# The low parts of the weight units are subtracted on GpSimd in place of VectorE, in a hybrid decoder layer

## The chip, the cores and the metric

One core of one Trainium2 chip runs the whole kernel. The metric is the device time of one execution in microseconds (us). TensorE (PE in the profile) multiplies matrices; VectorE (DVE), ScalarE (ACT) and GpSimd (POOL) do the elementwise work; SyncE (SP) and GpSimd issue most of the transfers between memory and SBUF. Each engine takes its instructions from a queue of its own, strictly in order; an instruction that has to wait holds all that stand behind it.

## What is computed

One layer for two groups of requests that share the weights: a prompt of 1024 positions and 8 sequences of 8 new positions, T = 1088 columns together. The model width is 1024, the feed-forward width 2816. Everything is float32.

```python
xn = rmsnorm(x)
q, k, v, a, b, gate_a, gate_b = split(xn @ w_in)           # 5632 columns
A = window_attention(q, k, v, sinks) @ w_o_attn            # 16 heads, 4 kv heads, window 128
u = a * sigmoid(b)
B = silu(layernorm(depthwise_conv31(u))) @ w_pb
h = x + (sigmoid(gate_a) * A + sigmoid(gate_b) * B) @ w_out
up = depthwise_conv3(rmsnorm(h) @ w_up)                    # 2 * 2816 columns
gate, val = split(up)
y = rmsnorm(h + (silu(gate) * val) @ w_down)
```

Key and value caches and convolution states are outputs as well.

## The kernel before

**How a product is made.** TensorE multiplies in a float format (`F32R`) that keeps fewer bits than float32. So each operand x is held as a pair: a high part, x rounded to that format, and a low part, x minus the high part. `mm3` (L188 to L192) makes a product from three matmuls into the same PSUM bank: high weight by high input (L190), high weight by low input (L191), and low weight by high input (L192). Of the three only L192 reads the low part of the weights, and it comes last.

**Weight units.** The weights arrive as units of 128x1024, each the weights for 128 output columns. A unit passes through four steps. `w_load` (L143) has it read from memory into a raw tile by SyncE's queue, two or three units ahead. `w_parts` (L156) makes the pair: ScalarE casts the raw tile to the high part (L171), and an engine subtracts the high part from the raw tile to give the low part (L172). The pair lies in one of two buffers that take turns (`slot`, L175), so a cast has to wait until TensorE has finished with the unit that held the buffer. `stream` (L194) then runs the three matmuls for all columns of the input, chunk by chunk. `weight` (L178) has the next unit split while the present one is multiplied: one unit ahead. `w_split` (L151) makes the split of a unit in two halves for the first five units (`FIRST = 5`), in one piece of 1024 columns for all others. Lines after L172 have a number higher by one in the kernel after the change.

**Stages.** The times are those of the profiled execution, rounded.

- 0 to 640 us: the input projection, 44 units in the order of `SEQUENCE`, 1088 columns each in chunks of 384, 384 and 320. Its results leave PSUM through small copies (L739 for q, for instance). Each of eight pairs of units b and a yields 128 channels for the long convolution, `conv` (L508), which is elementwise work on VectorE: some sixty operations of 512 columns (L520 and L526 to L542) for a group of 128 channels, here called a channel for short. At its end two DMA instructions of GpSimd's queue (L543, L544) store the result to `d_c`. The convolution is put behind more urgent work by 1200 steps of priority (`CONV_LATER`), so that it fills VectorE's gaps and comes late. In between, attention runs in units: scores on TensorE, `softmax` (L359) on VectorE and ScalarE with one small copy of the sinks on GpSimd (L362), transposes, and the product with the values.
- 640 to 736 us: the attention's output projection, 8 units, together with the layer norm of the convolution's result.
- 736 to 830 us and 831 to 930 us: the projections `w_pb` and `w_out`, 8 units each, and the second norm.
- 930 to 1003 us: the first three pairs of feed-forward up-projection units (`plain`), in quarters of 272 columns. Before each unit's results, `up_start` (L1144) has GpSimd clear and fill the edges of the tile (L1152); afterwards `finish` (L1175) runs the short convolution: `up_conv` copies two small edges on GpSimd (L1167 and the line after it), ScalarE makes the first tap (L1170), VectorE the other two (L1172), and GpSimd stores the product. VectorE also makes sums of the inputs (L1223) in this stretch, for what follows.
- 1003 to 1405 us: the other up-projection pairs, by a scheme with seven products of half-size blocks in place of eight. The weight blocks of this scheme are split by other lines (`split_ps`, L225 and L226), which the change does not touch; GpSimd negates a half tile here (L1196).
- 1405 to 1662 us: the down-projection and the last norm. Ten of its units are split by L171 and L172, again in tiles that other data held before; the rest by other lines.

**What sets the order.** The program is written in one sequence, and each instruction has a priority from its place in it. `later(off)` puts a block behind by so many places; `plan` and `tick` insert attention steps between matmuls. A scheduler then places the instructions in each engine's queue from these priorities and its own estimates of when operands are ready. So an instruction that changes its engine changes the order of its neighbours as well. Tiles that take turns in a buffer make an instruction wait for the last reader of the buffer.

Of the kernel before, what the change touches and what calls it, by code (L numbers as in the profile page):

```python
# [6 lines left out]
F32 = mybir.dt.float32  # L7
F32R = mybir.dt.float32r
AF = mybir.ActivationFunctionType
ALU = mybir.AluOpType  # L10
# [42 lines left out]
FIRST = 5  # L53
# [67 lines left out]
class Build:  # L121
# [34 lines left out]
    def w_parts(self, m):  # L156
        i = len(self.w_hl)
        r = self.w_raw[i]
        pool, x = self.slot(i)
        if pool is None:  # L160
            h, l = x
        else:
            th, tl = x if isinstance(x, tuple) else (f"whi{x}", f"wlo{x}")
            n = 2 if th == tl else 1
            h = self.t(pool, [P, DM], th, F32R, bufs=n)
            l = self.t(pool, [P, DM], tl, F32R, bufs=n)
        self.w_hl.append((h, l))

        def part(x):
            z = slice(x * DM // m, (x + 1) * DM // m)  # L170
            self.cast = self.nc.scalar.copy(h[:, z], r[:, z]).ins  # L171
            self.nc.vector.tensor_tensor(l[:, z], r[:, z], h[:, z].bitcast(F32), ALU.subtract)  # L172
        return [lambda x=x: part(x) for x in range(m)]

    def slot(self, i):  # L175
# [1502 lines left out]
```

## Time and profile before

| what | value |
|---|---|
| time of the runs | 1665.16 and 1667.07 us, median 1666.12 us |
| span of the profiled execution | 1662.4 us |
| TensorE busy | 1652.5 us (99%) |
| VectorE busy | 1337.3 us (80%) |
| ScalarE busy | 866.3 us (52%) |
| GpSimd busy | 290.2 us (17%) |
| mean DMA rate | 113 GB/s |

The span runs from the first to the last instruction that the profiler records. The rest of a run's time, 3.7 us of the median, lies outside it. A row of a timeline has the start in us, the duration in us, engine, line, operation, the tiles written and read, their shapes, how many instructions the row holds, and in brackets the time that the engine waited before it and what ended the wait. A row of a group has the line, engine, operation, tiles, shapes and count; behind the first bar the busy time in us and the mean of one in ns, behind the second the idle time of the engine just before these instructions.

### The profile page before, as it was taken

To read this page: it belongs to the slowest core of one execution; us is meant where nothing else is said; L and a number is where in the kernel's file an instruction comes from. 1 tells how busy PE (TensorE), PEld (TensorE's weight loads), DVE (VectorE), ACT (ScalarE), POOL (GpSimd) and SP (SyncE) were. 2 spreads that over 40 slices of the span, in tenths; PEclk is the share of its full clock that TensorE was granted. 3 is DMA by queue.
4 is the path that set the end of the run, shared out by engine and by line. 5 is a ranking of instruction groups with operands and counts; after the bars stand their busy time and mean duration, and the time that the engine had idled before them with its cause. 6 is when DMAs were issued, how large, how long until landed. Compare 5 with 4: busy or idle time off the path is not lost.

```text
span 1662.4 us, 29877 instructions
## 1 busy us (share of the span) xinstructions
PE 1652.5 (99%) x11550; PEld 1636.9 (98%) x11550; DVE 1337.3 (80%) x2432; ACT 866.3 (52%) x1781; POOL 290.2 (17%) x483
## 2 busy tenths in 40 slices
PE   9999999999999999999999999999999999999998
PEld 9999999999999999999999999999999999999997
DVE  7899979999989986855545896777887786988867
ACT  6424368774488845973233454444444454524222
POOL 0100112231011111110000171344444320000000
PEclk9999999999999999999999999999999999999999
DMA  6221212232121265544343332244444324766403
GB/s 208 84 71 42 75 60 81 99 103 86 55 53 48 77 227 168 178 154 145 106 155 108 80 125 103 97 113 115 112 114 111 94 103 134 243 168 168 118 14 108
DMA packets 98623, 187.09 MB, mean 113 GB/s; under 512 B 22848, under 2 KB 57680, under 8 KB 98464
## 3 DMA queue, kind: packets, MB, share of 16 engines
q1 hardware_dynamic: 79152, 125.18, 24.3%
q0 software_dynamic: 18896, 59.72, 11.9%
q8 instruction: 91, 1.49, 0.4%
q14 instruction: 52, 0.43, 0.1%
q10 hardware_dynamic: 432, 0.27, 0.1%
HBM read 129.75 MB, written 57.35 MB: 113 GB/s over the span
## 4 chain that ended last, share of the span: by engine, by line
PE 91%; DVE 5%; ACT 2%; DMA 1%; issue 1%; ACTq 0%; DVEq 0%; SPq 0%
PE mm L190 23%; PE mm L192 23%; PE mm L191 23%; PE aux L190 6%; PE aux L192 6%; PE aux L191 6%; PE aux L406 1%; DVE c L520 1%; PE aux L418 1%; PE aux L419 1%; PE aux L396 1%; PE aux L397 1%; DVE bt L520 1%; DVE q L739 1%; DMA bw<-d_b 0%
## 5 line engine op out<-in xcount | busy, mean ns | idle before, releaser
L190 PE MATMUL mm<-xh,whi 128*128 128x384 f32 (+1 forms) x904 | 301.1, 333 | 0.0
L191 PE MATMUL mm<-xl,whi 128*128 128x384 f32 (+1 forms) x904 | 295.4, 327 | 0.1
L192 PE MATMUL mm<-xh,wlo 128*128 128x384 f32 (+1 forms) x904 | 295.4, 327 | 0.0
L191 PEld LDWEIGHTS mm<-xl,whi 128*128 128x128 f32 x904 | 170.0, 188 | 1.6 <-DVE xl L277 0.7
L190 PEld LDWEIGHTS mm<-xh,whi 128*128 128x128 f32 x904 | 169.8, 188 | 0.7
L192 PEld LDWEIGHTS mm<-xh,wlo 128*128 128x128 f32 x904 | 169.7, 188 | 0.1
L190 PE MATMUL mm<-mh,whi 128*128 128x272 f32 (+4 forms) x428 | 125.9, 294 | 0.0
L191 PE MATMUL mm<-ml,whi 128*128 128x272 f32 (+4 forms) x428 | 125.1, 292 | 0.0
L192 PE MATMUL mm<-mh,wlo 128*128 128x272 f32 (+4 forms) x420 | 123.5, 294 | 0.0
L1172 DVE SCALAR_TENSOR_TENSOR acc<-st,fc,acc 128x1104 f32<-128x1104 f32 x88 | 119.8, 1364 | 2.8 <-ACT acc L1170 2.0
L171 ACT CAST whi<-wraw 128x1024 fp32r<-128x1024 f32 (+1 forms) x76 | 74.2, 981 | 79.8 <-PE mm L191 59.7
L520 DVE SCALAR_TENSOR_TENSOR bt<-u,consts,bt 128x513 f32<-128x513 f32 x120 | 89.8, 748 | 0.7
L520 DVE SCALAR_TENSOR_TENSOR c<-sm,hsum,c 128x512 f32<-128x512 f32 x120 | 89.6, 747 | 0.7
L172 DVE TENSOR_TENSOR wlo<-wraw,whi 128x1024 fp32r<-128x1024 f32 (+1 forms) x76 | 86.1, 1136 | 4.9 <-ACT whi L171 4.6
L520 DVE SCALAR_TENSOR_TENSOR c<-u,consts,c 128x512 f32<-128x512 f32 x112 | 83.7, 747 | 0.5
L190 PEld LDWEIGHTS mm<-mh,whi 128*128 128x128 f32 x428 | 80.5, 188 | 0.2
L191 PEld LDWEIGHTS mm<-ml,whi 128*128 128x128 f32 x428 | 80.6, 188 | 0.0
L192 PEld LDWEIGHTS mm<-mh,wlo 128*128 128x128 f32 x420 | 79.0, 188 | 0.0
L1152 POOL COPY st<-co 128x16 f32<-128x16 f32 x44 | 75.6, 1724 | 0.2 <-issue 0.2
L191 PE MATMUL mm<-tl,whi 128*128 128x272 f32 x240 | 69.6, 290 | 0.0
L1320 ACT COPY st<-mm 128x272 f32<-128x272 f32 (+2 forms) x133 | 44.6, 349 | 47.8 <-PE mm L192 47.8
L192 PE MATMUL mm<-th,whi 128*128 128x272 f32 x240 | 69.3, 289 | 0.0
(462 smaller groups left out, 5491.6 us busy)
## 6 DMA issues: line engine op xcount, KB each, us to landing
wraw<-wall SPq DMA_DIRECT2D x118, 512.0 KB, 3.8
bw<-d_b SPq DMA_DIRECT2D x42, 272.0 KB, 3.4
d_b<-gd POOLq DMA_DIRECT2D x36, 272.0 KB, 6.1
d_b<-acc POOLq DMA_DIRECT2D x24, 272.0 KB, 3.3
ar<-wdn SPq DMA_DIRECT2D x32, 192.0 KB, 4.3
d_g<-acc POOLq DMA_DIRECT2D x10, 544.0 KB, 4.3
ga<-d_ga SPq DMA_DIRECT2D x8, 544.0 KB, 4.0
gb<-d_gb SPq DMA_DIRECT2D x8, 544.0 KB, 3.6
```

Of the source, the lines that this page charges most:

```text
L171: self.cast = self.nc.scalar.copy(h[:, z], r[:, z]).ins
L172: self.nc.vector.tensor_tensor(l[:, z], r[:, z], h[:, z].bitcast(F32), ALU.subtract)
L190: mm(ps, wh, xh, start=first, stop=False, skip_group_check=more)
L191: mm(ps, wh, xl, start=False, stop=False, skip_group_check=more)
L192: mm(ps, wl, xh, start=False, stop=last, skip_group_check=more)
L396: nc.tensor.matmul(ps[:, j, :], q[g][:, h, qs], kd[g][:, keys], start=True, stop=False)
L397: nc.tensor.matmul(ps[:, j, :], q[g][:, h, qs], kl[g][:, keys], start=False, stop=True)
L406: nc.tensor.transpose(ps[:, h * P:(h + 1) * P], pt[:, h, kb * P:(kb + 1) * P], self.ident)
L520: mac = lambda o, x, w: nc.vector.scalar_tensor_tensor(o, x, w, o, ALU.mult, ALU.add)
L1152: nc.gpsimd.tensor_copy(ss[:, :, 0:2], co[:, f, 2:].rearrange("p (b t) -> p b t", b=NB))
L1172: nc.vector.scalar_tensor_tensor(acc, st[:, k:k + AW], fw(f, k), acc, ALU.mult, ALU.add)
L1320: op(d, r(ps))
```

## The change

From the sixth weight unit on, the low part is subtracted by GpSimd; the first five units stay on VectorE. Nothing else is edited: the same operands, the same tiles, the same cast on ScalarE.

```diff
         def part(x):
             z = slice(x * DM // m, (x + 1) * DM // m)
             self.cast = self.nc.scalar.copy(h[:, z], r[:, z]).ins
-            self.nc.vector.tensor_tensor(l[:, z], r[:, z], h[:, z].bitcast(F32), ALU.subtract)
+            low = self.nc.vector if i < FIRST else self.nc.gpsimd
+            low.tensor_tensor(l[:, z], r[:, z], h[:, z].bitcast(F32), ALU.subtract)
         return [lambda x=x: part(x) for x in range(m)]
```

Here `i` is the number of the unit in the order of use and `m` the number of pieces. 39 subtractions of the input projection, 24 of the three projections behind it, 6 of the first up-projection units and 10 of the down-projection change their engine: 79 operations of 128x1024.

## The prediction

> **What bounds the kernel now.** I read the page first, then TensorE's waits, then the windows of the stages in which VectorE is densest, then the timelines around each place where a moved subtraction gets a neighbour in its new queue.
>
> ```profile
> PE 1652.5 (99%) x11550; PEld 1636.9 (98%) x11550; DVE 1337.3 (80%) x2432; ACT 866.3 (52%) x1781; POOL 290.2 (17%) x483
> PE mm L629 <- DVE warm L622: 1.1, 1, 1.1
> PE mm L190 <- DVE H L1456: 0.9, 1, 0.9
> PE aux L418 <- ACT pth L225: 0.8, 1, 0.8
> 60.00:460.00 400.00, 399.90 (x2577) 395.60 (x2576) 372.26 (x698) 223.53 (x525) 61.20 (x120) 1.00 0.25 76
> 964.00:978.50 14.50, 14.50 (x117) 14.50 (x117) 14.50 (x24) 6.65 (x12) 10.81 (x2) 1.00 0.55 188
> ```
>
> TensorE (PE) is busy for 1652.5 of 1662.4 us: 9.9 us are idle in all, and none of its listed waits is over 1.1 us. So help to any other engine can win at most 9.9 us, 0.6%. A window's columns are its length, then PE, weight loads, VectorE (DVE), ScalarE (ACT) and GpSimd (POOL) busy, then PE's granted clock (1.00: full) and the DMA. VectorE comes next: 372.3 of 400 us from 60 to 460, and no pause at all from 964 to 978.5.
>
> ```profile
> L172 DVE TENSOR_TENSOR wlo<-wraw,whi 128x1024 fp32r<-128x1024 f32 x29 | 35.4, 1220 | 0.4 <-ACT whi L171 0.2
> 759.68 1.05 ACT L171 CAST whi<-wraw 128x1024 fp32r<-128x1024 f32 x1 [1.57 <-PE mm L191]
> 771.59 1.05 ACT L171 CAST whi<-wraw 128x1024 fp32r<-128x1024 f32 x1 [1.62 <-issue]
> ```
>
> The first row is the subtraction from 60 to 460 us: 29 of them at 1.22 us. The others are two casts, each made when PE leaves a weight buffer. Units follow at 11.9 us; less the cast, some 10.8 us remain to make the low part. That slack hides a slower subtraction if it starts when its cast ends.
>
> **The change, part by part.** The built program's order shows 79 subtractions of 128x1024 gone from VectorE's queue and the same 79 in GpSimd's. The matmuls stay; VectorE's and GpSimd's other work is placed anew around them.
>
> *One subtraction on GpSimd.* No row shows a two-input operation there. The nearest:
>
> ```profile
> 1076.91 0.69 DVE L226 TENSOR_TENSOR wlo<-wraw,wlo 128x512 fp32r<-128x512 f32 x1 [0.86 <-ACT wlo L225]
> 1077.23 1.81 POOL L1196 TENSOR_SCALAR gd<-acc 128x544 f32<-128x544 f32 x1
> 1077.52 0.43 DVE L1296 TENSOR_TENSOR st<-st,aux 128x272 f32<-128x272 f32 x1
> 966.68 2.63 DVE L1223 TENSOR_TENSOR s<-mh,ml 128x544 f32<-128x544 f32 x4
> 968.28 10.46 POOL L1167 COPY co<-st 128x2 f32<-128x2 f32 x1 [3.17 <-ACT st L1163]
> 978.62 1.37 DVE L1172 SCALAR_TENSOR_TENSOR acc<-st,fc,acc 128x1104 f32<-128x1104 f32 x1
> ```
>
> The scalar operation ends 1.43 us after VectorE's L226 (1076.91+0.69=1077.60 to 1079.04). For 1024 columns in place of 544 that is 2.7 us. Lower bound: VectorE's 1.22. Upper: 5.4, if a second input doubles it. I take 2.7, the row's own rate. The Trainium skill, "GPSIMD Engine Reference", section 3.1, gives 4497 ns for a two-input add of 2048 fp32 columns; 2.25 us for 1024 is an estimate by that page, and the sum below would be about 13 us in place of 24.
>
> *What the two engines cost each other.* A copy of two columns took 10.46 us at 968.28: VectorE ran two-input operations on SBUF without a gap, and the copy ended at 978.74, just after the first L1172. So GpSimd's reads wait for such a stream and get in ahead of an operation with per-partition scalars (L1172). The reverse, VectorE held by GpSimd, no row shows: the operations with one operand in PSUM (L1296) ran beside L1196 in 0.43 us, as elsewhere. Its bounds are nothing and the whole 2.7 us. By its nearest row, the copy, the exclusion is complete, so I take it as mutual. The Trainium skill says the same, "SBUF — State Buffer", section "Who interferes with whom": a VectorE instruction with two SBUF inputs contends with a GpSimd instruction that reads SBUF, and the later one fully blocks. The trace agrees for one direction (10.46 us); by that rule VectorE pays nearly the whole 2.7.
>
> ```profile
> L520 DVE SCALAR_TENSOR_TENSOR bt<-u,consts,bt 128x513 f32<-128x513 f32 x90 | 67.4, 748 | 0.6
> L520 DVE SCALAR_TENSOR_TENSOR c<-sm,hsum,c 128x512 f32<-128x512 f32 x90 | 67.2, 747 | 0.6
> L520 DVE SCALAR_TENSOR_TENSOR c<-u,consts,c 128x512 f32<-128x512 f32 x84 | 62.8, 747 | 0.5
> L526 DVE TENSOR_TENSOR c<-u,consts 128x992 f32<-128x992 f32 x12 | 14.2, 1185 | 0.1
> L528 DVE TENSOR_TENSOR sm<-u 128x527 f32<-128x527 f32 x6 | 4.2, 705 | 0.0
> L540 DVE TENSOR_TENSOR c<-c,bt 128x512 f32<-128x512 f32 x6 | 4.1, 687 | 0.0
> L542 DVE TENSOR_TENSOR u<-c,bt 128x512 f32<-128x512 f32 x6 | 4.1, 683 | 0.0
> ```
>
> From 60 to 460 us these steps with two SBUF inputs, all of the convolution, fill 224 of the 336.9 us (372.3 less 35.4) that VectorE keeps: two thirds. So the loss per subtraction lies between 1.8 (two thirds of 2.7) and 2.7 in this stage; I take the middle, 2.3, against 1.22 saved. VectorE gets busier, not freer.
>
> *First place: the sixth convolution channel.*
>
> ```profile
> 440.54 0.55 DVE L739 TENSOR_TENSOR q<-mm,q 64x384 fp32r<-64x384 f32 x1
> 444.14 0.34 PE L192 MATMUL mm<-xh,wlo 128*128 128x384 f32 x1
> 453.24 0.69 DVE L541 TENSOR_TENSOR u<-c 128x512 f32<-128x512 f32 x1
> 454.23 0.54 POOL L543 DMA_DIRECT2D d_c<-u  x1 [5.91 <-DVE u L541]
> ```
>
> In the new GpSimd queue the low part that PE needs at 444.14 stands behind this channel's two stores, and those wait for VectorE's L541, done at 453.9. Ahead of that L541 VectorE now has 40.1 us less (35.4 of 29 subtractions, 4.7 of 26 small operations placed later) and 29 holds more: at 2.3 us each 66.7. It can fill the 27.7 us that it idled: 453.9-40.1+66.7-27.7=452.8. Then 0.2 to start, 0.54 for the store, 2.7 for the subtraction: 456.2, PE 12 us late. With a hold of 1.8 the channel ends with the evacuation placed ahead of it (L739 at 440.54, then four short steps, 442.5), so PE is 1 or 2 us late; with 2.7 it is 24. Smaller collisions of this kind, with the first, second and fifth channels, lie inside the same delay, since PE that is late needs its weights later. Behind the waiting stores stand only the next subtractions and the next channel's memsets.
>
> *460 to 640 us.*
>
> ```profile
> 460.00:550.00 90.00, 89.15 (x580) 85.76 (x579) 81.19 (x194) 76.04 (x192) 12.39 (x25) 1.00 0.18 50
> 550.00:640.00 90.00, 90.00 (x568) 88.32 (x567) 73.79 (x144) 48.74 (x110) 14.93 (x29) 1.00 0.51 176
> L362 POOL COPY p<-nsink 128x4 f32<-128x4 f32 x32 | 14.1, 444 | 74.6 <-PE aux L406 69.9 <-ACT gt L222 4.1 <-PE mm L191 0.7
> ```
>
> VectorE has 25 us idle here; about twelve subtractions add 12x1.1=13: hidden, 0 (up to 10). The softmax's sink copies (L362) now queue behind subtractions, whose cover is the time PE gives to other matmuls: 2 us (0 to 8).
>
> *640 to 940 us.* Output projections: the slack of 10.8 us holds, and nothing late stands ahead in the queue: 0.
>
> *Second place: the first up-projection units.*
>
> ```profile
> 951.80 1.05 ACT L171 CAST whi<-wraw 128x1024 fp32r<-128x1024 f32 x1 [1.91 <-PE mm L191]
> 955.00 0.29 PE L192 MATMUL mm<-mh,wlo 128*128 128x272 f32 x1
> 953.28 1.31 ACT L1170 ACTIVATE acc<-st,fc 128x1104 f32<-128x1104 f32 x1
> 955.35 1.36 DVE L1172 SCALAR_TENSOR_TENSOR acc<-st,fc,acc 128x1104 f32<-128x1104 f32 x1
> 979.22 0.29 PE L192 MATMUL mm<-mh,wlo 128*128 128x272 f32 x1
> 981.80 1.37 DVE L1172 SCALAR_TENSOR_TENSOR acc<-st,fc,acc 128x1104 f32<-128x1104 f32 x1
> 985.63 1.22 DVE L172 TENSOR_TENSOR wraw<-wraw,wraw 128x1024 fp32r<-128x1024 f32 x1
> 986.76 2.77 DVE L1172 SCALAR_TENSOR_TENSOR acc<-st,fc,acc 128x1104 f32<-128x1104 f32 x2
> ```
>
> Here slack is small: cast done at 952.85, low part wanted at 955.00. VectorE streams, so the subtraction gets in ahead of the first L1172 (now as soon as ScalarE's L1170 is done, 954.6) and ends at 957.3: 2.3 us late. In the new queue the low part for 979.22 stands behind two such copies, a memset and three stores, one entry per L1172: the copies take those at 978.62 and 981.8, it takes the third (986.76; with the subtraction of 985.63 gone, at about 985.6), and ends at 988.3: 9 us late, which holds the first delay. Entry in an earlier gap: 5. One miss more: 16.
>
> *Third place, the down-projection.*
>
> ```profile
> 1399.39 1.23 DVE L172 TENSOR_TENSOR ml<-wraw,mh 128x1024 fp32r<-128x1024 f32 x1 [1.25 <-ACT mh L171]
> 1405.34 0.33 PE L192 MATMUL mm<-mh,whi 128*128 128x384 f32 x1
> ```
>
> Two subtractions follow each other from 1399.4: the second ends at 1404.8, wanted at 1405.34. I put 1 us (0 to 3).
>
> **Sum.** 12+0+2+9+1=24 us on the profiled execution's 1662.4: 1686.4. The runs' median, 1666.1, stands 3.7 above that span: **1690**.
>
> **Rivals.** *A, hidden:* at the input projection VectorE loses less than the 1.22 us it saves, so the sixth channel is done by 441 and nothing queues late; at the up-projection subtractions get in at once. Then VectorE's relief may take PE's 0.9 and 0.8 us waits too, and the sink copies cost 2 at most: 1664 to 1668, not slower. It decides at a hold below about 1.2 us. For it: the 10.8 us of slack, and no row with VectorE held. Against: the 10.46 us copy.
> *B, the subtraction is long:* 5.4 us with a hold of 4.6 gives 453.9-40.1+133-27.7=519 at the sixth channel, 78 us late with the longer subtraction; then 12x3.4-25=16, and 16 at the up-projection: 1776. Half-way from my case to that: 1735.
> *C, starved further:* two subtractions at the up-projection miss the L1172s and wait, as the copy at 968.28 did, 10.46 us each: 1690+21=1711. For it: that copy. Against: the sink copies (L362) between the convolution's steps took 444 ns on average.
> *D, relief pays:* all of PE's 9.9 us, 1656; but most of those lie in no wait for VectorE. The change cannot fail to do what it says: the queues show it.
>
> **Chances.** 2% (33 us, 1699.4 above and 1632.8 below) is about what a measurement of this kernel can tell from no change. Forecast 0.50, of which 0.41 lies within 2%; A 0.17; B 0.20, all slower; C 0.12, of which 0.02 within; D 0.01. Together: slower by over 2% 0.39, within 0.60, faster 0.01 as a bound on what I overlooked. The forecast's own range runs from its low ends together (1+0+0+5+0=6: 1672) to 1712, where the high ends no longer come together. For 8 in 10 it takes in A down to 1665 and B to 1745, a little past its half-way case.
>
> **What would show it.** Right: GpSimd busy up by 79x2.7=213 us or more, PE idle near 34 us, with waits of L192 matmuls for GpSimd around 455 and 980; L520 longer or later after a subtraction. Wrong: subtractions of 5 us, or PE without waits for GpSimd (A), or long subtraction spans outside the convolution (C).

## The result and the profile after

| | median of the runs | profiled span | PE busy | VectorE busy | GpSimd busy |
|---|---|---|---|---|---|
| before | 1666.12 us | 1662.4 us | 1652.5 us | 1337.3 us | 290.2 us |
| after | 1720.72 us | 1717.2 us | 1671.0 us | 1367.7 us | 481.6 us |

The changed kernel is slower: 1719.03 to 1722.41 us, ratio 1.0324 with a 95% interval of 1.0291 to 1.0356. That is 54.6 us more, where 23.9 were forecast. (To the kernel's description above: the first three units are split in quarters, not in halves; they keep their engine.)

These lines of the page of the changed kernel answer to those of before (lines of code from L173 on stand one lower than in the kernel before, so L521 is the convolution step that was L520):

```profile
PE 1671.0 (97%) x11550; PEld 1645.2 (96%) x11550; DVE 1367.7 (80%) x2353; ACT 866.1 (50%) x1781; POOL 481.6 (28%) x562
PE 69%; DVE 23%; ACT 5%; issue 2%; DMA 1%; POOL 0%; DVEq 0%; ACTq 0%; SPq 0%; POOLq 0%
L173 POOL TENSOR_TENSOR wlo<-wraw,whi 128x1024 fp32r<-128x1024 f32 x68 | 183.1, 2693 | 260.9 <-ACT whi L171 227.1
L521 DVE SCALAR_TENSOR_TENSOR bt<-u,consts,bt 128x513 f32<-128x513 f32 x120 | 111.4, 928 | 0.6
L521 DVE SCALAR_TENSOR_TENSOR c<-sm,hsum,c 128x512 f32<-128x512 f32 x120 | 101.9, 849 | 0.5
L521 DVE SCALAR_TENSOR_TENSOR c<-u,consts,c 128x512 f32<-128x512 f32 x112 | 97.3, 869 | 0.6
```

VectorE has 79 operations fewer and is busy 30.4 us longer. The convolution steps show where: the same instruction that took 748 or 747 ns on average now takes 849 to 928. The second line is the chain that ended last: VectorE has 23% of it, GpSimd nothing. In the kernel before VectorE had 5%:

```profile
PE 91%; DVE 5%; ACT 2%; DMA 1%; issue 1%; ACTq 0%; DVEq 0%; SPq 0%
```

Now TensorE's waits in the changed kernel:

```profile
PE aux L420 <- DVE ptl L227: 8.9, 7, 3.2
PE aux L562 <- DVE red L555: 6.1, 3, 2.3
PE aux L397 <- DVE ptl L227: 4.9, 3, 3.1
PE mm L191 <- ACT st L1164: 5.2, 2, 2.7
PE mm L191 <- ACT qs L745: 3.3, 3, 1.2
PE mm L191 <- DVE H L1457: 2.5, 5, 0.7
PE mm L193 <- POOL wlo L173: 0.8, 1, 0.8
```

The columns are the total in us, how often, and the longest. TensorE waited for a low part once, for 0.8 us. It waits for VectorE's attention steps (L227), for the layer norm's sums (L555), and for ScalarE's copies out of PSUM (L1164, L745).

**One hold.** The timelines of GpSimd and VectorE at 150 us:

```profile
150.05 2.76 POOL L173 TENSOR_TENSOR wlo<-wraw,whi 128x1024 fp32r<-128x1024 f32 x1 [11.99 <-ACT whi L171]
149.79 0.76 DVE L521 SCALAR_TENSOR_TENSOR bt<-u,consts,bt 128x513 f32<-128x513 f32 x1
150.47 2.89 DVE L521 SCALAR_TENSOR_TENSOR c<-u,consts,c 128x512 f32<-128x512 f32 x1
153.28 0.74 DVE L521 SCALAR_TENSOR_TENSOR c<-sm,hsum,c 128x512 f32<-128x512 f32 x1
```

The subtraction runs from 150.05 to 152.81. The convolution step that starts in this time takes 2.89 us in place of 0.75; the step behind it takes 0.74 again. VectorE was held for 2.1 us.

**Where the time went.** I compared each VectorE instruction that overlaps a subtraction with the median of the same instruction in the trace before; where it took over 0.3 us longer I call the difference a hold. The delay is the start of the same matmul in both traces, after less before, so it is exact for these two executions (stretches by the times of the trace before):

| stretch, us | subtractions | with a hold | holds, us | delay added, us | forecast, us |
|---|---|---|---|---|---|
| 60 to 460 | 30 | 23 | 46.9 | 24.8 | 12 |
| 460 to 640 | 11 | 8 | 13.6 | 9.3 | 2 |
| 640 to 736 | 7 | 7 | 14.3 | 8.6 | 0 |
| 736 to 930 | 17 | 13 | 24.5 | 0.0 | 0 |
| 930 to 1003 | 4 | 4 | 8.3 | 9.2 | 9 |
| 1003 to 1405 | 2 | 0 | 0 | 0.0 | 0 |
| 1405 to the end | 8 | 6 | 9.3 | 2.7 | 1 |
| sum | 79 | 61 | 116.9 | 54.6 | 24 |

Holds come at some 2 us each in all stretches but one. What they cost differs: nothing from 736 to 930, more than their length from 930 to 1003. Of the 2.7 us behind 1405 about half is no effect of the change: fill and only_pb_out (below), which have no GpSimd subtraction there, lose 1.3 and 1.4 us in this stretch against the same trace.

Of the 54.8 us by which the span grew, 36.3 are TensorE's idle time (46.2 in place of 9.9). Another 8.5 or so are a lower granted clock after such stops: 17 us at 0.50. The remaining ten lie in matmuls that the profile shows as longer; they were not taken apart.

### The profile page after: what moved, and what is told of

Same layout as the page of the kernel before. It is cut to its first block, busy times and chain, and to the rows that moved or that the text cites. A ratio compares the mean times of both kernels' runs of the same rounds, so it can differ in the third digit from the quotient of the medians.

```text
span 1717.2 us, 29881 instructions
## 1 busy us (share of the span) xinstructions
PE 1671.0 (97%) x11550; PEld 1645.2 (96%) x11550; DVE 1367.7 (80%) x2353; ACT 866.1 (50%) x1781; POOL 481.6 (28%) x562
## 4 chain that ended last, share of the span: by engine, by line
PE 69%; DVE 23%; ACT 5%; issue 2%; DMA 1%; POOL 0%; DVEq 0%; ACTq 0%; SPq 0%; POOLq 0%
PE mm L191 16%; PE mm L193 16%; PE mm L192 16%; DVE c L521 6%; PE aux L191 5%; PE aux L193 5%; PE aux L192 5%; DVE bt L521 4%; DVE s L1224 1%; ACT p L374 1%; DVE q L740 1%; DVE c L527 1%; DVE p L369 1%; DVE c L528 1%; PE aux L407 1%
## 5 line engine op out<-in xcount | busy, mean ns | idle before, releaser
L173 POOL TENSOR_TENSOR wlo<-wraw,whi 128x1024 fp32r<-128x1024 f32 x68 | 183.1, 2693 | 260.9 <-ACT whi L171 227.1
L1173 DVE SCALAR_TENSOR_TENSOR acc<-st,fc,acc 128x1104 f32<-128x1104 f32 x88 | 124.1, 1411 | 13.3 <-ACT acc L1171 12.4
L521 DVE SCALAR_TENSOR_TENSOR bt<-u,consts,bt 128x513 f32<-128x513 f32 x120 | 111.4, 928 | 0.6
L521 DVE SCALAR_TENSOR_TENSOR c<-sm,hsum,c 128x512 f32<-128x512 f32 x120 | 101.9, 849 | 0.5
L521 DVE SCALAR_TENSOR_TENSOR c<-u,consts,c 128x512 f32<-128x512 f32 x112 | 97.3, 869 | 0.6
L374 ACT ACTIVATE p<-p,nm 128x257 f32<-128x257 f32 (+1 forms) x128 | 62.3, 490 | 23.2 <-DVE nm L369 20.9
L1153 POOL COPY st<-co 128x16 f32<-128x16 f32 x44 | 71.7, 1636 | 0.2 <-issue 0.2
```

Source lines behind the costliest of these rows:

```text
L173: low.tensor_tensor(l[:, z], r[:, z], h[:, z].bitcast(F32), ALU.subtract)
L374: nc.scalar.activation(pt[:, j, lo:width + 1], pt[:, j, lo:width + 1], AF.Exp, bias=nm[:, j:j + 1], scale=-1.0, accum_out=den[:, j:j + 1])
L521: mac = lambda o, x, w: nc.vector.scalar_tensor_tensor(o, x, w, o, ALU.mult, ALU.add)
L1153: nc.gpsimd.tensor_copy(ss[:, :, 0:2], co[:, f, 2:].rearrange("p (b t) -> p b t", b=NB))
L1173: nc.vector.scalar_tensor_tensor(acc, st[:, k:k + AW], fw(f, k), acc, ALU.mult, ALU.add)
```

## The experiments

The theory after the first look: a GpSimd instruction that reads SBUF holds a VectorE instruction with two inputs from SBUF until it is done, and the held time reaches TensorE through VectorE's fixed queue (**holds**). The rivals: VectorE's queue was placed anew by the scheduler, 515 of its 2294 entries other than the subtractions, and the new order is worse (**order**); or low parts come late in GpSimd's queue (**queue**). The first three kernels take these apart two by two: the old and the new order on VectorE, each with GpSimd reading and not reading.

**fill**: new order, no reads.

```diff
-            low = self.nc.vector if i < FIRST else self.nc.gpsimd
-            low.tensor_tensor(l[:, z], r[:, z], h[:, z].bitcast(F32), ALU.subtract)
+            if i < FIRST:
+                self.nc.vector.tensor_tensor(l[:, z], r[:, z], h[:, z].bitcast(F32), ALU.subtract)
+            else:
+                self.nc.gpsimd.memset(l[:, z].bitcast(F32), 0.0)
```

> In place of the subtraction GpSimd fills the low part with zeros (units from the sixth on): it writes the same tile but reads nothing, so the low parts of these weights are left out of the result. VectorE's queue is that of the changed kernel, with 9 of 2294 entries elsewhere. Theory 1, holds (a GpSimd subtraction reads SBUF and holds VectorE's operations that have two SBUF inputs): no read, no hold, so the 54.6 us vanish: 1660 to 1669 us. Theory 2, order (VectorE's queue was placed anew, 515 of 2294 entries, and its evacuations of PSUM now stand behind convolution steps): the order is still there, so 1700 to 1725 us. Theory 3, queue (the low part comes late in GpSimd's queue, behind stores): a fill is shorter than a subtraction but stands at the same place, so about half of the loss, 1680 to 1700 us.

**twice**: old order, reads that nobody waits for (the diff is against the kernel before).

```diff
             self.nc.vector.tensor_tensor(l[:, z], r[:, z], h[:, z].bitcast(F32), ALU.subtract)
+            if i >= FIRST:
+                self.nc.gpsimd.tensor_tensor(r[:, z], r[:, z], h[:, z].bitcast(F32), ALU.subtract)
```

> VectorE subtracts as in the kernel before, in nearly its order (25 of 2294 entries elsewhere), and GpSimd then makes the same subtraction once more, into the raw tile that nobody reads any more. No matmul waits for GpSimd. Theory 1, holds: VectorE keeps its 79 subtractions (some 96 us) and pays the holds besides (the trace of the changed kernel shows some 115 us of them), so at least the loss of the changed kernel: 1720 to 1800 us, likeliest 1745. Theory 2, order: nothing is placed anew, 1664 to 1675 us. Theory 3, queue: nobody waits for these subtractions, 1664 to 1675 us.

**clear**: old order, no reads; the added line is `self.nc.gpsimd.memset(r[:, z], 0.0)`.

> The control of the run twice: VectorE subtracts as before, and GpSimd then fills the raw tile with zeros in place of the second subtraction. The same place in both queues and the same order on VectorE as in twice, but nothing is read. All theories: 1664 to 1672 us. If it is slower, it is GpSimd's queue (the stores and copies behind the fills) or the raw tiles that come free later, and not the reads.

Measured: fill 1665.99 us (ratio 1.0000, 0.9991 to 1.0009), twice 1752.04 (1.0517, 1.0499 to 1.0536), clear 1675.55 (1.0052, 1.0037 to 1.0067). Reads decide, in either order; order and queue alone cost nothing in fill. The groups and the page of fill show both halves of it:

```profile
L175 POOL MEMSET wlo<- 128x1024 f32 x68 | 65.4, 968 | 341.0 <-PE mm L195 290.2 <-PE aux L195 28.6 <-PE aux L194 11.9
L523 DVE SCALAR_TENSOR_TENSOR bt<-u,consts,bt 128x513 f32<-128x513 f32 x120 | 89.7, 748 | 0.6
```

```profile
PE 1653.7 (99%) x11550; PEld 1637.6 (98%) x11550; DVE 1255.2 (75%) x2353; ACT 867.6 (52%) x1781; POOL 341.4 (21%) x562
```

The convolution step is back at 748 ns; the 186 VectorE instructions that overlap a fill took under 0.2 us longer in all. And VectorE is relieved by 82 us (1255.2 against 1337.3) without any gain: TensorE idled for only 9.9 us in the kernel before, 2.0 of them in listed waits for VectorE (1.1 and 0.9). A fill is also shorter (0.97 us on average against 2.69), so fill alone leaves a late low part (queue) possible; twice rules it out, since nobody waits for its second subtraction.

One hold does not fit the theory's wording. At 63.39 us an instruction with a single tile as input, which takes 0.17 us in the kernel before, was held as well, beside a subtraction that ran from 61.25 to 65.77 (in only_in and short_gpsimd it took 2.41 and 2.40 us):

```profile
63.39 2.41 DVE L636 TENSOR_SCALAR nsink<-consts 128x16 f32<-128x16 f32 x1
```

So 60 of the 61 held instructions have two inputs from SBUF, but that is not the whole condition.

clear missed its expectation by 3.6 us. Its loss is one stop; the row of the waits, and TensorE's and SyncE's rows of the timeline:

```profile
PE mm L192 <- ACT whi L227: 7.6, 1, 7.6
```

```profile
1010.70 0.60 PE L192 MATMUL mm<-mh,whi 128*128 128x272 f32 x1 [7.63 <-ACT whi L227]
1003.32 1.75 SPq L148 DMA_DIRECT2D wraw<-wall  x4
```

TensorE waits at 1003 us for a weight block whose load was issued at 1003.32. The extra write to the raw tiles is what these kernels have beside the kernel before; which wait ahead of the load it lengthened was not tried. twice has a stop of the same kind (6.2 us for a cast), and loses 8.9 of its 86 us from 1003 to 1405, where it lies.

**only_in, only_mid, only_up, only_pb_out**: GpSimd only for the units of one stage; the condition in the changed line becomes `FIRST <= i < self.n_in`, then the 24 units behind `n_in`, the 6 units behind those, and of the 24 the last 16.

> GpSimd subtracts only the 39 units of the input projection; the other 40 are VectorE's again. By the two traces PE lags by 34 us at the end of this stage in the changed kernel, and the rest comes later. Theory 1, holds: the loss is local, so the 34 us stay and the later ones go: 1696 to 1704 us. Theory 3, queue: the waits behind the convolution's stores lie in this stage alone, so nearly the whole loss stays only if the later stages have none: 1700 to 1720 us. By the prediction's own sum (12+0+2): 1680 us.

> GpSimd subtracts only the 24 units of the three projections after the input projection; VectorE's order is the kernel before's but for 2 entries. The two traces put 8.6 us here in the changed kernel, all during the layer norm's steps (PE waits for L555's sums). If holds on those steps are the cause: 1672 to 1677 us. By the prediction (0 in this stage): 1665 to 1668 us.

> GpSimd subtracts only the six units of the first up-projection pairs; VectorE's order is the kernel before's but for 21 entries. The two traces put 9.2 us here in the changed kernel, the prediction 9. If it is this stage's own loss: 1673 to 1677 us. If it came from the changed kernel's order or from what the earlier delay left behind: 1665 to 1669 us. If PE waits for the low part (the prediction's step), the trace shows waits of L193 for GpSimd; if holds are the cause, waits of L191 for ScalarE's evacuations behind VectorE's sums.

> GpSimd subtracts only the 16 units of the two projections from 736 to 930 us. In the changed kernel VectorE is held there by 24.5 us in 13 holds, as much per subtraction as elsewhere, and PE loses nothing. All theories: 1664 to 1668 us. If PE loses here, the loss read off by stages is not local.

Measured: only_in 1703.51 us (1.0224, 1.0208 to 1.0239), only_mid 1674.63 (1.0047, 1.0031 to 1.0064), only_up 1673.97 (1.0045, 1.0030 to 1.0060), only_pb_out 1665.50 (0.9999, 0.9990 to 1.0009). Against the runs of before beside each, that is 37.9, 8.5, 7.8 and 0 us. With the 2.7 of the down-projection the first three make 56.9, against 54.6 for the whole change: the loss is local to its stages. The waits of only_mid and then of only_up:

```profile
PE aux L562 <- DVE red L555: 6.1, 3, 2.3
```

```profile
PE mm L191 <- ACT st L1164: 5.2, 2, 2.7
PE mm L193 <- POOL wlo L173: 0.8, 1, 0.8
```

They are the changed kernel's own waits at these places, with VectorE's old order but for 2 and 21 entries. And in only_pb_out, the timelines of GpSimd and VectorE, and then the window of the stage in which this lies, show a hold that costs nothing:

```profile
796.13 2.38 POOL L173 TENSOR_TENSOR wlo<-wraw,whi 128x1024 fp32r<-128x1024 f32 x1 [9.48 <-ACT whi L171]
796.42 2.51 DVE L227 TENSOR_TENSOR ml<-mar,mh 128x48 fp32r<-128x48 f32 x2 [0.30 <-ACT mh L226]
799.29 0.56 DVE L1019 TENSOR_TENSOR gb<-mm,gb 128x384 f32<-128x384 f32 x1 [0.36 <-PE mm L193]
```

```profile
736.00:830.00 94.00, 94.00 (x572) 94.00 (x571) 54.05 (x94) 32.00 (x64) 19.62 (x10) 1.00 0.41 141
```

Two small subtractions take 2.51 us, yet the next entry still finds TensorE's result not ready (0.36 us of idle time): VectorE is busy for 54 of 94 us here, by the window, and makes up for the hold. TensorE is busy for all 94.

**pieces and half**: does the length of a hold count, or the sum? In pieces the GpSimd subtraction runs as four of 256 columns; in half VectorE subtracts the first 512 columns and GpSimd the other 512.

```diff
+                for y in range(0, DM, DM // 4):
+                    y = slice(y, y + DM // 4)
+                    self.nc.gpsimd.tensor_tensor(l[:, y], r[:, y], h[:, y].bitcast(F32), ALU.subtract)
```

> The changed kernel, with each GpSimd subtraction cut in four of 256 columns; VectorE's queue keeps the changed kernel's order to the last entry. Theory length (PE loses because one urgent VectorE operation, an evacuation or an attention step, is held for some 2.0 us at once, longer than the lead that it has): a piece holds at most some 0.6 us and VectorE goes on between pieces, so most of the 54.6 us go: 1675 to 1692 us. Theory sum (PE loses because VectorE loses about 1.5 us a subtraction in all, however it is cut): the sum stays, or grows by the pieces' starts: 1715 to 1735 us.

> Each of the 79 units in halves: VectorE subtracts 512 columns, GpSimd the other 512. A GpSimd operation is half as long, and VectorE is relieved by half as much. Theory length: holds of some 1.0 us against leads of 1 to 2 us, so much less than half of the loss: 1670 to 1685 us. Theory sum: half of the loss, 1690 to 1697 us.

Measured: pieces 1712.36 us (1.0276, 1.0260 to 1.0291), half 1683.85 (1.0108, 1.0093 to 1.0123). Neither theory holds in its plain form: pieces lies just below the range of the sum, half inside that of the length. The holds are 70 us in pieces and 67 in half (117 in the changed kernel), 18 of the 67 on VectorE's own halves of the subtractions; the losses are 46 and 18. So nearly the same sum of holds cost very different times. half's queue differs from the changed kernel's in 267 entries, and it loses nothing at 930 to 1003; how much of that is order, and how much the shape of the holds, is open. The first lines of the pages of pieces and of half:

```profile
PE 1669.0 (98%) x11550; PEld 1644.6 (96%) x11550; DVE 1325.2 (78%) x2353; ACT 865.2 (51%) x1781; POOL 563.3 (33%) x799
PE 1659.2 (98%) x11550; PEld 1637.1 (97%) x11550; DVE 1362.9 (81%) x2432; ACT 865.2 (51%) x1781; POOL 407.7 (24%) x562
```

In pieces VectorE is busy for 12 us less than in the kernel before, and the kernel is 46 us slower. In half it is busy for 38 us more than in pieces, and the loss is 28 us smaller. A balance of VectorE's busy time doesn't foretell the loss.

**short_vector and short_gpsimd**: the kernel before and the changed one with a third of the convolution's steps, so that VectorE has far less to do in the input projection.

```diff
-        for j in range(1, 16):
+        for j in range(1, 6):
```

> The kernel before with 10 of the 15 steps of each convolution channel left out (the taps from the eleventh on are missing from its result), so that VectorE has about 175 us less to do in the input projection: from 60 to 460 us it is left with some 60% of the time. The base of the run short_gpsimd. Every theory: VectorE is not the bound, so 1660 to 1667 us.

> The changed kernel with the same shortened convolution as short_vector. Theory balance (the input projection loses because VectorE is nearly full there and the holds use up its idle time, as the prediction's sum had it): with 40% idle the 34 to 38 us of this stage go, and 8.5 + 7.8 + 2.5 = 19 us of the later stages stay: 1680 to 1688 us. Theory chain (a hold costs where TensorE waits for an operation just behind it, an evacuation or an attention step, however idle VectorE is on the whole): a large part of the 34 to 38 us stays, fewer only as fewer convolution steps are there to be held: 1692 to 1715 us.

Measured: short_vector 1665.66 us (1.0003, 0.9993 to 1.0012 against before), short_gpsimd 1692.84 (1.0161, 1.0142 to 1.0180), by the ranges at the lower edge of the chain theory. The stages decide, not the total. The windows from 60 to 460 us, first of short_vector and then of short_gpsimd:

```profile
60.00:460.00 400.00, 400.00 (x2578) 395.81 (x2577) 258.29 (x525) 224.56 (x525) 56.02 (x120) 1.00 0.26 76
```

```profile
60.00:460.00 400.00, 398.77 (x2564) 393.82 (x2563) 245.61 (x492) 221.43 (x522) 127.78 (x149) 1.00 0.25 76
```

Up to 460 us short_gpsimd falls 2.2 us behind short_vector, and 4.3 up to 640 (24.8 and 34.1 in the full kernel), while half of the holds are still there (23.3 us up to 460 in place of 46.9). So in the input projection the loss falls by far more than the holds do when VectorE has a third of its time free: how full it is matters most there, as the balance theory said. The total came out higher because of the later stages: 8.1, 9.1 and 7.7 us, the last of them 5 us more than I had put. About 2 us of that excess are the profiled execution's own, which took 1695.24 us against the median of 1692.84; the rest is not explained.

The delays of the main kernels, worked out as above (short_gpsimd against short_vector), in us at the end of each stretch:

| | 460 | 640 | 736 | 930 | 1003 | end | holds in all |
|---|---|---|---|---|---|---|---|
| after | 24.7 | 34.0 | 42.6 | 42.6 | 51.8 | 54.6 | 117 |
| fill | 0.0 | -0.1 | 0.3 | 0.3 | 0.8 | 2.2 | 0 |
| twice | 37.0 | 44.3 | 55.9 | 55.8 | 62.6 | 85.4 | 100 |
| pieces | 13.6 | 21.4 | 27.4 | 27.4 | 36.7 | 45.4 | 70 |
| short_gpsimd | 2.2 | 4.3 | 12.4 | 12.4 | 21.5 | 29.2 | 86 |

twice has fewer holds than the changed kernel and loses more. Its VectorE still makes all the subtractions, so it is fuller; that this is the reason was not shown by itself.

## Why the prediction was right or wrong

**Right: the side, the hold, the price of a subtraction.** The 79 subtractions took 212.2 us, against 213 forecast (2.69 us on average, 2.38 at the least). GpSimd's busy time rose by 191.4 only, since its other work took 21 us less, 17 of them in the two edge copies (L1168 and L1169). VectorE is held by GpSimd: fill and twice show it. The Trainium skill ("SBUF — State Buffer", "Who interferes with whom") says that a GpSimd instruction that only writes SBUF doesn't contend with a VectorE instruction of two SBUF inputs; the trace of fill agrees, with under 0.2 us over 186 overlaps. Rival A (hidden) fell with the holds, rival B with the price, and rival C did not come: the longest subtraction took 5.25 us. The path from the hold to TensorE was wrong: of the waits for GpSimd that were forecast around 455 and 980 us, one of 0.8 us came.

**Too large: the hold.** I took 2.3 us per subtraction in the convolution's stage. It is 46.9/30 = 1.6: 7 of 30 held nothing, and where an instruction was held, part of the subtraction had already run.

**The step that failed: the idle time.** The working at the sixth channel let VectorE "fill the 27.7 us that it idled", and from 460 to 640 us set 13 us of losses against 25 us of idle time and put 0. With the measured holds the channel's sum would be 453.9-40.1+46.9-27.7=433.0, early enough for TensorE to be 1 or 2 us late by the prediction's own rule. In the trace the channel ended at 465.5, later even than the sum without the credit (460.7), and TensorE was 25 us late. So the hold that was taken too large hid part of the error. The window of the same matmuls in the changed kernel:

```profile
60.00:485.00 425.00, 408.47 (x2578) 397.11 (x2577) 386.07 (x674) 223.46 (x526) 145.05 (x150) 1.00 0.22 71
```

VectorE is busy for 386 us, less than the 400 that the stage had, and the stage still takes 425: VectorE now idles for 39 us. None of the 27.7 us was filled. My reading: idle time in a queue of fixed order lies where the next entry waits for TensorE; when TensorE is late, that wait moves along and can't be filled. What a hold delays instead is the short operation that stands behind the convolution steps. The stop at 227.6 us, VectorE's and TensorE's rows:

```profile
227.97 0.73 DVE L521 SCALAR_TENSOR_TENSOR bt<-u,consts,bt 128x513 f32<-128x513 f32 x1
228.63 0.73 DVE L521 SCALAR_TENSOR_TENSOR c<-sm,hsum,c 128x512 f32<-128x512 f32 x1
229.29 0.24 DVE L540 TENSOR_SCALAR u<-c,consts 128x64 f32<-128x64 f32 x1
229.45 0.68 DVE L541 TENSOR_TENSOR c<-c,bt 128x512 f32<-128x512 f32 x1
230.06 0.67 DVE L227 TENSOR_TENSOR ptl<-aux,pth 128x512 fp32r<-128x512 f32 x1
230.78 0.50 PE L420 MATMUL aux<-ptl,v 128*128 128x512 f32 x1 [3.20 <-DVE ptl L227]
```

No instruction here is held. VectorE is behind by what 11 earlier holds (23.1 us, less the subtractions that it was spared) left, works without a pause, and reaches the attention's L227 too late; TensorE waits 3.2 us. fill has this order, but for 9 entries, and no such stop. The attention's waits for L227 (8.9 and 4.9 us) are the largest part of TensorE's listed waits. Idle time does protect where there is far more of it (142 of 400 us in short_vector; short_gpsimd lost 2.2 there), but it isn't used up one for one. From 460 to 640 us it is the same: the holds (13.6 us) are less than the idle time (25), and TensorE loses 9.3.

**The term of the sixth channel, 12 us: real, but paid already.** GpSimd's and TensorE's rows:

```profile
465.78 0.54 POOL L544 DMA_DIRECT2D d_c<-u  x1 [1.95 <-DVE u L543]
466.34 2.42 POOL L173 TENSOR_TENSOR wlo<-wraw,whi 128x1024 fp32r<-128x1024 f32 x1
469.18 0.34 PE L193 MATMUL mm<-xh,wlo 128*128 128x384 f32 x1
```

The low part did stand behind the channel's store and ended at 468.76, 24.6 us after its old time of need (444.14). TensorE asked for it at 469.18, since it was 25 us late by other waits. I had seen that delays at one place hold each other, and had not looked for the larger one.

**640 to 940 us, 0 against 8.6.** I checked the slack of the low parts, and it did hold. I didn't check VectorE's own chains: each of three layer-norm sums is a few two-input operations, and TensorE waits for the last (6.1 us in three waits; the clock at 0.50 behind the second adds 1.7).

**The up-projection, 9 against 9.2: the amount right by luck, the way wrong.** I had TensorE waiting for low parts. It waited 0.8 us for one, and 5.2 us for ScalarE's copies. GpSimd's, VectorE's, ScalarE's and TensorE's rows, and two windows:

```profile
1011.85 5.15 POOL L173 TENSOR_TENSOR wlo<-wraw,whi 128x1024 fp32r<-128x1024 f32 x1
1014.03 4.31 DVE L1224 TENSOR_TENSOR s<-s,s 128x544 f32<-128x544 f32 x3
1017.62 0.65 ACT L226 CAST th<-s 128x544 fp32r<-128x544 f32 x1 [2.19 <-DVE s L1224]
1024.74 0.65 ACT L226 CAST th<-s 128x544 fp32r<-128x544 f32 x1 [3.12 <-DVE s L1224]
1025.29 0.38 ACT L1164 COPY st<-mm 128x272 f32<-128x272 f32 x1
1025.72 0.39 PE L191 MATMUL mm<-mh,whi 128*128 128x272 f32 x1 [2.43 <-ACT st L1164]
```

```profile
1022.00:1026.00 4.00, 1.57 (x13) 1.35 (x11) 4.00 (x7) 0.93 (x2) 0.00 (x0) 1.00 0.00 0
1030.00:1034.00 4.00, 4.00 (x20) 4.00 (x19) 3.96 (x4) 1.92 (x3) 4.00 (x2) 0.50 0.00 0
```

The three sums at 1014.03 take 4.31 us beside the subtraction; three of this size take 1.99 elsewhere (993.63). A cast waits for them at 1017.62. Some seven us later the copy that frees a PSUM bank (L1164) still stands behind a cast that waits for VectorE's next sums (L1224), which come late, and TensorE stops for 2.43 us. VectorE has no pause there (4.00 of 4 us in the window), so 8.3 us of holds become 8 to 9 of delay. Each part of this was in the trace before; I followed GpSimd's queue and not who stands behind VectorE on ScalarE.

## What to carry to other kernels

Before work goes to GpSimd, ask what VectorE runs at that moment: beside operations with two SBUF inputs, an engine that is "only 17% busy" stops one that is 93% busy. Price a hold not against an engine's idle total but against the first urgent entry behind it, and follow the wait through the third engine's queue; the same 2 us cost nothing where VectorE was busy for 54 of 94 us and their full length where it had no pause. And relief of an engine that the bound engine isn't waiting for gained nothing: 82 us less on VectorE, ratio 1.0000.

## What the runs showed of the hardware that was not expected

TensorE's granted clock falls to half after short stops. It was 0.50 for some 3.4 us behind single stops of 2.1, 3.1 and 2.3 us (from 362, 563.5 and 737.6 us on), and for 6.8 us around the stops of 2.4 and 2.7 us (from 1027.7 on). The first of these:

```profile
362.20:365.40 3.20, 3.20 (x14) 3.20 (x13) 2.61 (x5) 1.17 (x2) 0.19 (x1) 0.50 0.14 57
```

The Trainium skill ("TensorE: Matmul & The Clock Gate", "What's actually happening") has the clock halved after an idle window of about 3.4 us; here single stops below that were enough, and one of 3.2 us at 227.6 left it at 1.00. A fill of 128x1024 takes 0.97 us on GpSimd on average, and a subtraction 2.38 at the least in the changed kernel; cut in four, each piece takes 0.71 at the least.
